# Weight sums of a hybrid decoder block: from loads, VectorE and stores to accumulating DRAM-to-DRAM transfers on GpSimd's queue

## The chip, the core and the metric

The kernel runs on one core of a Trainium2 chip. The metric is the device time of one execution in microseconds. The kernel before takes 1697.17 us, the median of three runs (1697.14 to 1698.39).

The engines are called as the profile calls them: PE (TensorE matmul) and PEld (its weight loads), DVE (VectorE), ACT (ScalarE), POOL (GpSimd) and SP (SyncE). SP, ACT and POOL each have a queue from which transfers (DMAs) are issued in program order; all of them are carried out by the core's 16 DMA engines. "Idle before" and "who waited" in the views are inferred from semaphore events.

## The reference, cut to what matters

One layer of a decoder block on 256 positions of width 2048, in float32: a pre-norm, one wide projection, dilated attention and a gated recurrence side by side, gates, an output projection, and then the feed-forward part, with a normalisation and a residual sum behind each half:

```
a = rmsnorm(h, norm_mix_pre)
proj = a @ w_in                                   # 2048 x 17408
q_a, k_a, v_a, q_r, f_r, i_r, g_r, gate_a, gate_r = split_columns(proj)
attn  = dilated_window_attention(...)             # 3 groups of 8 heads
r_out = hgrn2_chunked(...)                        # 8 heads
y = sigmoid(gate_a) * (attn @ w_attn_branch) + sigmoid(gate_r) * (r_out @ w_hgrn_branch)
h = h + rmsnorm(y @ w_mix_out, norm_mix_post)
a = rmsnorm(h, norm_ffn_pre)
gt, up = split(a @ w_ffn_gate_up)                 # 2048 x 11264
ff = (silu(gt) * up) @ w_ffn_down                 # 5632 x 2048
h = h + rmsnorm(ff, norm_ffn_post)
```

## The kernel before

**Products.** All the large matrix products stream their weights from DRAM. Each weight tile is split into a high and a low part (`hi` on ACT, `lo` on DVE: `raw - hi`), and so are the activations; a product is three matmuls: high by high, high by low, low by high (`prod`, L461).

**Steps and items.** A `Wide` block covers 2 x 512 output columns. It is computed in steps; a step takes 256 rows of the weight, so its `raw` tile is four quarters of 128 x 512 (two row halves k by two column groups g), 1 MB in all, loaded by SP as two DMAs of 512 KB (`load_wide`, L274) into one of three `raw` buffers. `Block`s are narrower; their chunks of 512 KB are loaded by `load_pair` (L262), two to a `raw` buffer. `items` lists all steps and chunks in order of use: 64 steps of the eight early wide blocks (items 0 to 63), 176 chunks, 16 steps of the output projection, 88 of gate and up, 44 of down. The main loop at the end runs over the items: `prepare` (L337) splits the item two ahead and issues loads up to three further `raw` buffers, `multiply` issues the matmuls of this item, and then the evacuations and the side work (`lanes`: attention and recurrence) advance by one piece each. Every engine runs its own queue in the order in which the loop wrote it; nothing but semaphores ties an engine to the item that the loop was at.

**The start.** x (2 MB, in five DMAs) and the first weight tiles are loaded on SP's queue in turn. In the first block the activations of step c + 1 are transposed on PE halfway through step c (`more_x`, L766), and ACT and DVE split them (L617, L621). ACT takes its work in order: the weights of a step, two squares of the norm (L688), then these activations. Between the two sides of a step stand twelve matmuls.

**Seven products.** In some steps a 2 x 2 block product is made with seven products in place of eight (21 matmuls for 24, less adds). It needs four sums of the weight quarters and four sums of the activations (`seven_sums`, L517), and the results are put together in `gather` (L506) and by one add for each output tile when a block is done (L815, L1199, L1405, L1454). With `by7 == 1` the weight sums are made on DVE when the step is split (L434, L440, L441). With `by7 == 2`, which holds for 20 steps of gate and up (`GATE_UP3`, `GATE_UP4`), the sums are made ahead and kept in DRAM, in tiles `presum` of 128 x 2048; `fetch_sums` (L319) loads them four items before their step.

**Sums made ahead.** `weight_sums` (L294) is a generator, advanced once per chunk item by `ahead_of_time` (L327), once the pool `fp` is open and the recurrence doesn't hold it. For each of the 20 jobs it loads the four quarters into an SBUF tile `pre` with two DMAs on SP's queue, makes the sums with four DVE operations (L309, L310, L312, L313), and stores them with one 1 MB DMA on ACT's queue (L316). `make_room` (L1543) finishes what is left of it before the pools of the feed-forward part open.

**POOL.** GpSimd has little to do: it fills constants, issues two small DMAs of `rowg` (L173, L174), and fills the tile `at` of each half of the recurrence with zeros (L987). DVE writes the diagonal of `at` later (L1009).

Of the kernel before, what the change touches and what calls it, by code (L numbers as in the profile page):

```python
# [14 lines left out]
F32 = mybir.dt.float32  # L15
# [3 lines left out]
OP = mybir.AluOpType  # L19

P = 128
# [79 lines left out]
def tile_hybrid_block(ctx: ExitStack, tc: tile.TileContext, t, out):  # L101
    nc = tc.nc
# [12 lines left out]
    def nm(s):  # L115
        serial[0] += 1
        return f"{s}_{serial[0]}"
# [22 lines left out]
    def rsqrt_mean(dst, ss, n, bias=None):  # L140
# [44 lines left out]
    dram = ctx.enter_context(  # L185
        tc.tile_pool(name="dram", bufs=1, space=bass.MemoryType.DRAM, reuse_waits="tile")
    )
# [12 lines left out]
    fp = []  # L200
# [92 lines left out]

    def weight_sums(jobs):  # L294

        for n in jobs:
            x = fp[0].tile([P, 2048], F32, tag="pre", bufs=1, name=nm("pre"))
            b, i = steps[n][:2]
            m = b.order[i][0]
            for g in range(2):  # L300
                nc.sync.dma_start(
                    x[:, g * 1024 : (g + 1) * 1024].rearrange("p (k c) -> p k c", k=2),
                    b.w[2 * m * P : (2 * m + 2) * P, b.cols[g] : b.cols[g] + 512]
                    .rearrange("(k p) c -> p k c", p=P),
                )
            for _ in range(4):
                yield
            r = [x[:, q * 512 : (q + 1) * 512] for q in range(4)]
            nc.vector.tensor_sub(r[2], r[2], r[0])  # L309
            nc.vector.tensor_sub(r[0], r[1], r[0])  # L310
            yield
            nc.vector.tensor_add(r[1], r[1], r[2])  # L312
            nc.vector.tensor_sub(r[3], r[3], r[1])  # L313
            yield
            pre[n] = dram.tile([P, 2048], F32, name=nm("presum"))
            nc.scalar.dma_start(pre[n], x)  # L316
            yield

    def fetch_sums(i):  # L319
        if i < len(items) and items[i][0] is steps:  # L320
# [5 lines left out]

    def ahead_of_time():  # L327

        if fp and back and not hold[0]:
            advance(back)  # L330

    def split(i):
        if i < len(items):
# [67 lines left out]
    def split_wide(n):  # L401

        b, i, raw = steps[n][:3]
        m, by7 = b.order[i]
        prep = b.prep(m, by7) if b.prep else iter(())
        next(prep, None)
        if (b, i) == spare:
            hi = p3("spare", F32R, 2048, 1, "sum")
            lo = Joined(p3("spare", F32R, 1536, 4, "d"), p3("spare", F32R, 512, 4, "d"))
            nc.scalar.activation(hi, raw, AF.Copy)  # L410
            for c in (slice(0, 1536), slice(1536, 2048)):
                nc.vector.tensor_sub(lo[:, c], raw[:, c], hi[:, c].bitcast(F32))
            steps[n][3] = hi, lo
            return
        hi, lo = wslot(), p3("wl", F32R, 2048, 3)
        if not by7:
            for c in (slice(0, 1024), slice(1024, 2048)) if b.halves else (slice(0, 2048),):
                nc.scalar.activation(hi[:, c], raw[:, c], AF.Copy)  # L418
                next(prep, None)
                nc.vector.tensor_sub(lo[:, c], raw[:, c], hi[:, c].bitcast(F32))  # L420
            steps[n][3] = hi, lo
            return
        d = raw[:, 512:]
        if by7 == 2:
            for c, x in zip((slice(0, 1024), slice(1024, 2048)), pre_in.pop(n)):
                nc.scalar.activation(hi[:, c], x, AF.Copy)
                nc.vector.tensor_sub(lo[:, c], x, hi[:, c].bitcast(F32))
            dhi, dlo = p3("dh", F32R, 1536, 4, "d"), p3("dl", F32R, 1536, 4, "d")
            nc.scalar.activation(dhi, d, AF.Copy)
            nc.vector.tensor_sub(dlo, d, dhi.bitcast(F32))  # L430
            steps[n][3] = hi, lo, dhi, dlo
            return
        s = p3("sum", F32, 2048, 1)
        nc.vector.tensor_sub(  # L434
            s[:, :1024].rearrange("p (a c) -> p a c", a=2),
            raw[:, 512:1536].rearrange("p (a c) -> p a c", a=2),
            raw[:, None, :512].to_broadcast([P, 2, 512]),
        )
        nc.scalar.activation(hi[:, :1024], s[:, :1024], AF.Copy)  # L439
        nc.vector.tensor_add(s[:, 1024:1536], raw[:, 512:1024], s[:, 512:1024])  # L440
        nc.vector.tensor_sub(s[:, 1536:], raw[:, 1536:], s[:, 1024:1536])  # L441
        nc.scalar.activation(hi[:, 1024:], s[:, 1024:], AF.Copy)
        next(prep, None)
        dhi, dlo = p3("dh", F32R, 1536, 4, "d"), p3("dl", F32R, 1536, 4, "d")
        nc.scalar.activation(dhi, d, AF.Copy)  # L445
        for c in (slice(0, 1024), slice(1024, 2048)):
            nc.vector.tensor_sub(lo[:, c], s[:, c], hi[:, c].bitcast(F32))  # L447
        next(prep, None)
        nc.vector.tensor_sub(dlo, d, dhi.bitcast(F32))  # L449
        steps[n][3] = hi, lo, dhi, dlo  # L450
# [55 lines left out]
    def gather(b):  # L506
# [7 lines left out]
        nc.vector.tensor_add(e[1, 1], x["p7"], e[1, 1])  # L514
        b.rest = e

    def seven_sums(f, dst):  # L517

        s = ptile("s").rearrange("p (n t) -> p n t", n=4)
        a11, a12, a21, a22 = f[:, 0, :P], f[:, 1, :P], f[:, 0, P:], f[:, 1, P:]  # L520
        for o, x, c, y in ((0, a21, -1.0, a22), (1, s[:, 0, :], -1.0, a11)):
            nc.vector.scalar_tensor_tensor(
                out=s[:, o, :], in0=x, scalar=c, in1=y, op0=OP.mult, op1=OP.subtract
            )
        nc.vector.tensor_sub(s[:, 2, :], a11, a21)
        nc.vector.tensor_sub(s[:, 3, :], a12, s[:, 1, :])
        return (
            lambda: nc.scalar.activation(dst[:, 0], s, AF.Copy),
            lambda: nc.vector.tensor_sub(dst[:, 1], s, dst[:, 0].bitcast(F32)),
        )  # L530
# [120 lines left out]
    def advance(q):  # L651
        if q:
            try:
                next(q[0])
            except StopIteration:
                q.popleft()
                return

    def flush(q):
        while q:  # L660
            advance(q)
# [146 lines left out]
    def totals(b, then):  # L808

        while "r1c" not in ready:  # L810
            yield
        keys = ((0, 0), (0, 1), (1, 0), (1, 1))
        if b.rest:
            for key in keys:
                nc.vector.tensor_add(b.rest[key], b.bank[key], b.rest[key])  # L815
            yield
        for key in keys:
            then(key, b.rest[key] if b.rest else b.bank[key])
            if key == (0, 1):
                yield  # L820
# [374 lines left out]
            nc.scalar.dma_start(hx[j], xv[:, :, j * 512 : (j + 1) * 512])  # L1195

    def mix_sum(j, i, b):
        f = b.rest[i, j % 2]
        nc.vector.tensor_add(f, b.bank[i, j % 2], f)  # L1199

    def mix_square(j, i, b):
        sq = zss[0][:, 4 * i + j : 4 * i + j + 1]
# [197 lines left out]
        turns.append(u)  # L1400

    def evac_ffn(b):
        e, x = b.rest, b.bank
        for key in ((0, 0), (0, 1), (1, 0), (1, 1)):
            nc.vector.tensor_add(e[key], x[key], e[key])  # L1405
            s, g = key
            if g == 0:
                nc.scalar.activation(e[key], e[key], AF.Silu, scale=r2c[:, s : s + 1])
        yield
        for s in range(2):  # L1410
            nc.vector.tensor_mul(e[s, 1], e[s, 1], e[s, 0])
        turns.append([e[0, 1], e[1, 1]])
# [34 lines left out]

    def down_sum(j, i, b):

        f = b.rest[i, j % 2]  # L1450
        nc.vector.tensor_add(f, b.bank[i, j % 2], f)  # L1451

    def down_square(j, i, b):
        sq, r2 = fss[0][:, 4 * i + j : 4 * i + j + 1], r2c[:, i : i + 1]  # L1454
# [88 lines left out]
    def make_room(c):  # L1543
        if c == 2:
            flush(evacs)
            flush(back)
            end_phase1()

    early = [
# [76 lines left out]
    for i in range(len(items)):  # L1626
        kind, n, _ = items[i]
        b, c = kind[n][:2]
        wide = kind is steps
        if wide:  # L1630
            now[0] = b
        if c == 0 and b.pre:
            b.pre()
        if not wide and n in items_pre:
            items_pre[n]()
        if together <= i < together + 5:
            if i == together:
                flush(evacs)
                mix_to_ffn(i)
            continue  # L1640
        if not (wide and b.mid):
            prepare(i)
        if i >= len(items) - 3:
            continue
        multiply(i)
        if b.post:
            b.post(c)
        if wide and c == b.last7:
            gather(b)
        advance(evacs)  # L1650
        if wide and c == b.turn:
            flush(evacs)
            turn_act(turns.popleft())
        for _ in range(2):
            if turns and type(turns[0]) is not list:
                advance(turns)
        advance_lanes()
        if not wide:
            ahead_of_time()
        if c == (len(b.order) if wide else b.steps) - 1:  # L1660
            evacs.append(b.evac(b if wide else b.banks))
            if wide:
                advance(evacs)
# [63 lines left out]
```

## Time and profile before

| what | us |
|---|---|
| median of the runs | 1697.17 |
| profiled execution, from its first to its last instruction (span) | 1695.7 |
| PE busy | 1684.4 |
| DVE busy | 1416.2 |
| ACT busy | 945.6 |
| POOL busy | 3.8 |

Only the span is known of the profiled execution itself; the runs were timed from outside, and their median is 1.5 us above it. PE's matmuls are pipelined, so the busy time of one (some 390 ns for 512 columns) is longer than the step from one to the next; the number of matmuls in a stretch tells the rate. The DMA share is the mean busy share of the 16 DMA engines; in the page it stands at 5 to 8 tenths in most slices.

### The profile page before, as it was taken

To read this page: it belongs to the slowest core of one execution; us is meant where nothing else is said; L and a number is where in the kernel's file an instruction comes from. 1 tells how busy PE (TensorE), PEld (TensorE's weight loads), DVE (VectorE), ACT (ScalarE), POOL (GpSimd) and SP (SyncE) were. 2 spreads that over 40 slices of the span, in tenths; PEclk is the share of its full clock that TensorE was granted. 3 is DMA by queue.
4 is the path that set the end of the run, shared out by engine and by line. 5 is a ranking of instruction groups with operands and counts; after the bars stand their busy time and mean duration, and the time that the engine had idled before them with its cause. 6 is when DMAs were issued, how large, how long until landed. Compare 5 with 4: busy or idle time off the path is not lost.

```text
span 1695.7 us, 21719 instructions
## 1 busy us (share of the span) xinstructions
PE 1684.4 (99%) x8257; PEld 1415.9 (83%) x8257; DVE 1416.2 (84%) x1623; ACT 945.6 (56%) x1080; POOL 3.8 (0%) x13
## 2 busy tenths in 40 slices
PE   9999999999999999999999999999999999999997
PEld 7888888888888888888888888888888888888886
DVE  6999888867978987776668888888888888898987
ACT  6655555544455555555545547555555555665653
POOL 0000000000000000000000000000000000000000
PEclk9999999999999999999999999999999999999999
DMA  8567666669677766788857646777777777777673
GB/s 286 204 224 243 231 232 229 234 216 316 228 250 256 261 239 215 259 310 279 291 171 276 208 165 226 270 249 251 255 254 255 250 248 272 252 269 259 238 255 130
DMA packets 228905, 413.49 MB, mean 244 GB/s; under 512 B 12816, under 2 KB 79552, under 8 KB 226240
## 3 DMA queue, kind: packets, MB, share of 16 engines
q1 hardware_dynamic: 218544, 373.93, 65.6%
q10 hardware_dynamic: 10192, 38.15, 5.9%
q8 instruction: 64, 1.05, 0.3%
q14 instruction: 41, 0.34, 0.1%
q0 software_dynamic: 64, 0.02, 0.0%
HBM read 376.92 MB, written 35.13 MB: 243 GB/s over the span
## 4 chain that ended last, share of the span: by engine, by line
PE 98%; DVE 1%; ACT 0%; issue 0%; DVEq 0%; ACTq 0%
PE acc L138 62%; PE aux L138 34%; PE aux L943 0%; PE aux L610 0%; PE aux L1374 0%; DVE fz L1501 0%; PE acc L1374 0%; DVE wl L420 0%; ACT junk L1455 0%; PE aux L597 0%; DVE e L1451 0%; ACT w L418 0%; PE aux L1136 0%; PE aux L1246 0%; DVE yT L578 0%
## 5 line engine op out<-in xcount | busy, mean ns | idle before, releaser
L138 PE MATMUL acc<-xT,w 128*128 128x256 f32 (+1 forms) x2048 | 365.1, 338 | 0.0
L420 DVE TENSOR_TENSOR wl<-raw,w 128x2048 fp32r<-128x2048 f32 (+1 forms) x140 | 304.6, 2183 | 70.5 <-ACT w L418 68.7
L138 PEld LDWEIGHTS acc<-xT,w 128*128 128x128 f32 x2048 | 311.9, 188 | 44.7
L365 DVE TENSOR_TENSOR w<-raw,w 128x1024 fp32r<-128x1024 f32 x176 | 215.1, 1223 | 118.1 <-ACT w L364 117.5
L418 ACT ACTIVATE w<-raw 128x2048 fp32r<-128x2048 f32 (+1 forms) x140 | 254.6, 1827 | 104.4 <-PE aux L138 33.6
L364 ACT ACTIVATE w<-raw 128x1024 fp32r<-128x1024 f32 x176 | 185.8, 1058 | 191.9 <-PE acc L138 135.8
L138 PE MATMUL acc<-w,xT 128*128 128x512 f32 x578 | 168.8, 391 | 0.0
L439 ACT ACTIVATE w<-sum 128x1024 fp32r<-128x1024 f32 x57 | 60.6, 1062 | 184.8 <-DVE sum L434 177.6
L138 PE MATMUL acc<-w,hT 128*128 128x512 f32 x472 | 152.7, 391 | 0.4 <-DVE hT L1258 0.4
L447 DVE TENSOR_TENSOR wl<-sum,w 128x1024 fp32r<-128x1024 f32 x114 | 137.2, 1221 | 12.8 <-ACT w L439 12.8
L138 PEld LDWEIGHTS acc<-w,xT 128*128 128x128 f32 x578 | 108.2, 188 | 22.2
L138 PE MATMUL aux<-w,hT 128*128 128x512 f32 x374 | 120.0, 389 | 0.0
L449 DVE TENSOR_TENSOR dl<-raw,dh 128x1536 fp32r<-128x1536 f32 x57 | 100.1, 1757 | 14.3 <-ACT dh L445 13.0
L138 PE MATMUL aux<-w,xT 128*128 128x512 f32 x344 | 109.8, 389 | 0.0
L138 PEld LDWEIGHTS acc<-w,hT 128*128 128x128 f32 x472 | 88.5, 188 | 19.0 <-DVE hT L1258 0.9
L138 PE MATMUL acc<-wl,hT 128*128 128x512 f32 x236 | 91.9, 389 | 0.0
L445 ACT ACTIVATE dh<-raw 128x1536 fp32r<-128x1536 f32 x57 | 84.1, 1476 | 8.0 <-PE aux L138 4.4
L138 PE MATMUL acc<-w,a 128*128 128x512 f32 x268 | 83.6, 389 | 0.0
L138 PEld LDWEIGHTS aux<-w,hT 128*128 128x128 f32 x374 | 70.2, 188 | 14.5
L138 PE MATMUL acc<-w,so 128*128 128x512 f32 x240 | 80.8, 391 | 0.0
L138 PE MATMUL aux<-w,a 128*128 128x512 f32 x254 | 79.4, 389 | 0.0
L138 PEld LDWEIGHTS aux<-w,xT 128*128 128x128 f32 x344 | 64.6, 188 | 13.4
(299 smaller groups left out, 2976.2 us busy)
## 6 DMA issues: line engine op xcount, KB each, us to landing
raw<-in_w_in SPq DMA_DIRECT2D x270, 512.0 KB, 4.8
raw<-in_w_ffn_gate_up SPq DMA_DIRECT2D x156, 512.0 KB, 4.9
raw<-in_w_ffn_down SPq DMA_DIRECT2D x88, 512.0 KB, 5.5
pre<-in_w_ffn_gate_up SPq DMA_DIRECT2D x40, 512.0 KB, 6.5
presum<-pre ACTq DMA_DIRECT2D x20, 1024.0 KB, 4.7
s<-presum SPq DMA_DIRECT2D x40, 512.0 KB, 6.9
raw<-in_w_mix_out SPq DMA_DIRECT2D x32, 512.0 KB, 4.8
act<-acts SPq DMA_DIRECT2D x22, 512.0 KB, 6.6
```

The costliest lines, as they stand in the source:

```text
L138: nc.tensor.matmul(ps, lhsT, rhs, start=start, stop=stop, skip_group_check=True)
L364: nc.scalar.activation(wh, raw, AF.Copy)
L365: nc.vector.tensor_sub(wl, raw, wh.bitcast(F32))
L418: nc.scalar.activation(hi[:, c], raw[:, c], AF.Copy)
L420: nc.vector.tensor_sub(lo[:, c], raw[:, c], hi[:, c].bitcast(F32))
L439: nc.scalar.activation(hi[:, :1024], s[:, :1024], AF.Copy)
L445: nc.scalar.activation(dhi, d, AF.Copy)
L447: nc.vector.tensor_sub(lo[:, c], s[:, c], hi[:, c].bitcast(F32))
L449: nc.vector.tensor_sub(dlo, d, dhi.bitcast(F32))
```

## The change

`weight_sums` no longer uses SBUF, DVE, SP or ACT. Each of the 20 jobs is four stages of DMAs on GpSimd's queue, of 128 x 512 (256 KB) each, all from DRAM to DRAM:

- `begin`: four copies of weight quarters into `presum`,
- `first`: two DMAs that add a quarter of the weight to one of `presum`,
- `second` and `third`: one each, adding one quarter of `presum` to another.

The jobs are interleaved: job n's `begin` is issued with job n - 1's `first`, n - 2's `second` and n - 3's `third`, and the next such group eight advances later. The generator is advanced in every item from the ninth on (`i > 7`), wide ones too, so that its instructions are written among items 8 to 191; before, they were written among the chunk items. There are 160 DMAs, 40 MB written.

The scheme of seven products is one whose weight sums are all additions, since the DMAs add. To make up for it `seven_sums` changes signs in the sums of the activations (the same number of operations), and at the end of a block two of the four output tiles are `bank - rest` in place of `bank + rest` (`complete`). The sums made on DVE for `by7 == 1` change from subtractions to additions in the same places. The flush in `make_room` goes.

```diff
     def weight_sums(jobs):
 
-        for n in jobs:
-            x = fp[0].tile([P, 2048], F32, tag="pre", bufs=1, name=nm("pre"))
+        def pieces(n):
             b, i = steps[n][:2]
             m = b.order[i][0]
-            for g in range(2):
-                nc.sync.dma_start(
-                    x[:, g * 1024 : (g + 1) * 1024].rearrange("p (k c) -> p k c", k=2),
-                    b.w[2 * m * P : (2 * m + 2) * P, b.cols[g] : b.cols[g] + 512]
-                    .rearrange("(k p) c -> p k c", p=P),
-                )
-            for _ in range(4):
+            return [
+                b.w[(2 * m + k) * P : (2 * m + k + 1) * P, b.cols[g] : b.cols[g] + 512]
+                for g, k in product(range(2), repeat=2)
+            ]
+
+        def begin(n):
+            r = pieces(n)
+            x = pre[n] = dram.tile([P, 2048], F32, name=nm("presum"))
+            for at, q in ((0, 0), (1, 1), (2, 0), (3, 3)):
+                nc.gpsimd.dma_start(x[:, at * 512 : (at + 1) * 512], r[q])
+
+        def first(n):
+            r, x = pieces(n), pre[n]
+            nc.gpsimd.dma_start(x[:, :512], r[1], accum_op=OP.add)
+            nc.gpsimd.dma_start(x[:, 1024:1536], r[2], accum_op=OP.add)
+
+        def second(n):
+            x = pre[n]
+            nc.gpsimd.dma_start(x[:, 512:1024], x[:, 1024:1536], accum_op=OP.add)
+
+        def third(n):
+            x = pre[n]
+            nc.gpsimd.dma_start(x[:, 1536:], x[:, 512:1024], accum_op=OP.add)
+
+        stages = (begin, first, second, third)
+        for at in range(len(jobs) + 3):
+            for lag in (3, 2, 1, 0):
+                if 0 <= at - lag < len(jobs):
+                    stages[lag](jobs[at - lag])
+            for _ in range(8):
                 yield
-            r = [x[:, q * 512 : (q + 1) * 512] for q in range(4)]
-            nc.vector.tensor_sub(r[2], r[2], r[0])
-            nc.vector.tensor_sub(r[0], r[1], r[0])
-            yield
-            nc.vector.tensor_add(r[1], r[1], r[2])
-            nc.vector.tensor_sub(r[3], r[3], r[1])
-            yield
-            pre[n] = dram.tile([P, 2048], F32, name=nm("presum"))
-            nc.scalar.dma_start(pre[n], x)
-            yield
...
     def ahead_of_time():
 
-        if fp and back and not hold[0]:
-            advance(back)
+        advance(back)
...
+    def complete(b, key):
+
+        add_to = nc.vector.tensor_add if key[1] else nc.vector.tensor_sub
+        add_to(b.rest[key], b.bank[key], b.rest[key])
...
         a11, a12, a21, a22 = f[:, 0, :P], f[:, 1, :P], f[:, 0, P:], f[:, 1, P:]
-        for o, x, c, y in ((0, a21, -1.0, a22), (1, s[:, 0, :], -1.0, a11)):
-            nc.vector.scalar_tensor_tensor(
-                out=s[:, o, :], in0=x, scalar=c, in1=y, op0=OP.mult, op1=OP.subtract
-            )
+        nc.vector.tensor_sub(s[:, 0, :], a22, a21)
         nc.vector.tensor_sub(s[:, 2, :], a11, a21)
-        nc.vector.tensor_sub(s[:, 3, :], a12, s[:, 1, :])
+        nc.vector.scalar_tensor_tensor(
+            out=s[:, 1, :], in0=s[:, 0, :], scalar=-1.0, in1=a11, op0=OP.mult, op1=OP.subtract
+        )
+        nc.vector.tensor_add(s[:, 3, :], a12, s[:, 1, :])
...
         if c == 2:
             flush(evacs)
-            flush(back)
             end_phase1()
...
         advance_lanes()
-        if not wide:
+        if i > 7:
             ahead_of_time()
```

In the order of the instructions, POOL's queue before reads as follows from its last constants on to its end. `rowg` holds three small vectors, `at` is the tile of the recurrence; the brackets name the semaphores that an instruction waits for (DMAHW: earlier DMAs of SP and ACT; Activation, DVE, PE: those engines).

```order
L170 MEMSET eps 128x1
L173 DMA rowg<-in_norm_ffn_pre 16x128
L174 DMA rowg<-in_hgrn_lower_bounds 16x128
L987 MEMSET at_3359 128x1024 [waits DMAHW6_49,DMAHW4_49,DMAHW7_49,DMAHW2_49,Activation_49]
L987 MEMSET at_4554 128x1024
L1723 UNCONDITIONAL_BRANCH
```

In the change the same place reads as follows (DMASW: earlier DMAs of POOL's own queue, eight semaphores in turn; each `presum` is a job).

```order
L170 MEMSET eps 128x1
L173 DMA rowg<-in_norm_ffn_pre 16x128
L174 DMA rowg<-in_hgrn_lower_bounds 16x128
L308 DMA presum_660<-in_w_ffn_gate_up 128x512 x4
L312 DMA presum_660<-in_w_ffn_gate_up 128x512 [waits DMASW2_49]
L313 DMA presum_660<-in_w_ffn_gate_up 128x512 [waits DMASW4_49]
L308 DMA presum_963<-in_w_ffn_gate_up 128x512 [waits DMASW0_49]
L308 DMA presum_963<-in_w_ffn_gate_up 128x512 [waits DMASW1_49]
L308 DMA presum_963<-in_w_ffn_gate_up 128x512
L308 DMA presum_963<-in_w_ffn_gate_up 128x512 [waits DMASW3_49]
L317 DMA presum_660<-presum_660 128x512 [waits DMASW7_49]
```

The four copies of the first job stand right behind the DMAs of `rowg` and wait for nothing; what follows waits for POOL's own DMAs alone. Further on in POOL's queue, the first fill of `at` now stands behind 81 of the 160 DMAs, and 40 more stand between it and the second fill:

```order
L313 DMA presum_3198<-in_w_ffn_gate_up 128x512 [waits DMASW1_49]
L308 DMA presum_3395<-in_w_ffn_gate_up 128x512
L308 DMA presum_3395<-in_w_ffn_gate_up 128x512 [waits DMASW0_49]
L308 DMA presum_3395<-in_w_ffn_gate_up 128x512
L308 DMA presum_3395<-in_w_ffn_gate_up 128x512 [waits DMASW2_49]
L1003 MEMSET at_3421 128x1024 [waits DVE_49,PE_49]
L321 DMA presum_3002<-presum_3002 128x512 [waits DMASW4_49,DMASW3_49]
```

So the fills, which stood next to each other, moved behind the transfers, and the transfers behind the fills wait for them. On SP's queue the 40 loads of `pre` are gone from among the loads of chunks, and nothing else moved:

```order
-L269 DMA raw_2758<-in_w_in 128x4x256 x2
-L301 DMA pre_2789<-in_w_ffn_gate_up 128x2x512 x2
-L269 DMA raw_2814<-in_w_in 128x4x256 x2
-L269 DMA raw_2867<-in_w_in 128x4x256 x2
-L269 DMA raw_2912<-in_w_in 128x4x256 x2
-L301 DMA pre_2963<-in_w_ffn_gate_up 128x2x512 x2
```

These are rows of before as the difference prints them; the loads of `raw` stand in the change too, in the same order under other numbers. PE's order of matmuls and weight loads is the same row for row.

More of the change, by code (lines that the diff above doesn't have):

```diff
@@ L433, in split_wide @@
         s = p3("sum", F32, 2048, 1)
-        nc.vector.tensor_sub(
+        nc.vector.tensor_add(
             s[:, :1024].rearrange("p (a c) -> p a c", a=2),
@@ L440, in split_wide @@
         nc.vector.tensor_add(s[:, 1024:1536], raw[:, 512:1024], s[:, 512:1024])
-        nc.vector.tensor_sub(s[:, 1536:], raw[:, 1536:], s[:, 1024:1536])
+        nc.vector.tensor_add(s[:, 1536:], raw[:, 1536:], s[:, 1024:1536])
         nc.scalar.activation(hi[:, 1024:], s[:, 1024:], AF.Copy)
@@ L814, in totals @@
             for key in keys:
-                nc.vector.tensor_add(b.rest[key], b.bank[key], b.rest[key])
+                complete(b, key)
             yield
@@ L1197, in mix_sum @@
     def mix_sum(j, i, b):
-        f = b.rest[i, j % 2]
-        nc.vector.tensor_add(f, b.bank[i, j % 2], f)
+        complete(b, (i, j % 2))
     def mix_square(j, i, b):
@@ L1402, in evac_ffn @@
     def evac_ffn(b):
-        e, x = b.rest, b.bank
+        e = b.rest
         for key in ((0, 0), (0, 1), (1, 0), (1, 1)):
-            nc.vector.tensor_add(e[key], x[key], e[key])
+            complete(b, key)
             s, g = key
@@ L1448, in down_sum @@
     def down_sum(j, i, b):
-        f = b.rest[i, j % 2]
-        nc.vector.tensor_add(f, b.bank[i, j % 2], f)
+        complete(b, (i, j % 2))
     def down_square(j, i, b):
```

## The prediction

> **What bounds the kernel now.** I read the page first: the span, the busy shares, and the chain that ended last.
>
> ```profile
> span 1695.7 us, 21719 instructions
> PE 1684.4 (99%) x8257; PEld 1415.9 (83%) x8257; DVE 1416.2 (84%) x1623; ACT 945.6 (56%) x1080; POOL 3.8 (0%) x13
> ...
> PE 98%; DVE 1%; ACT 0%; issue 0%; DVEq 0%; ACTq 0%
> ```
>
> PE is busy for all but 11.3 us of the span, and 98% of the chain is its own matmuls. The view of waits, for PE alone, says what there is to save:
>
> ```profile
> PE aux L138 <- DVE warm L162: 1.2, 1, 1.2
> PE acc L138 <- DVE hT L1258: 0.4, 1, 0.4
> PE acc L138 <- DVE gate L1173: 0.2, 1, 0.2
> PE aux L943 <- DVE p L937: 0.2, 1, 0.2
> ```
>
> After the first 1.2 us PE waits 0.8 us for anything. Relief for DVE, ACT or SP can bring that much at the most. So the question is only whether the change makes PE wait where it does not now, and by its nature it can do so through the DMA engines. The third view is busy time by stretch; the last columns are the granted clock, the DMA share and GB/s.
>
> ```profile
> 0.00:5.00 5.00, 3.81 (x10) 1.28 (x11) 0.27 (x1) 1.28 (x1) 2.00 (x11) 1.00 0.56 177
> 5.00:10.00 5.00, 5.00 (x23) 3.54 (x24) 3.15 (x8) 3.56 (x8) 0.00 (x0) 1.00 0.96 319
> 10.00:15.00 5.00, 5.00 (x24) 4.13 (x23) 3.72 (x5) 2.92 (x4) 0.00 (x0) 1.00 1.05 393
> 15.00:20.00 5.00, 5.00 (x25) 3.99 (x24) 3.33 (x4) 3.59 (x9) 0.00 (x0) 1.00 1.05 387
> 20.00:25.00 5.00, 5.00 (x26) 4.13 (x25) 3.75 (x8) 4.77 (x9) 0.00 (x0) 1.00 1.05 384
> 25.00:30.00 5.00, 5.00 (x26) 4.15 (x25) 3.07 (x7) 3.31 (x11) 0.00 (x0) 1.00 0.88 288
> 60.00:345.00 285.00, 285.00 (x1259) 236.00 (x1258) 252.02 (x221) 159.86 (x133) 0.00 (x0) 1.00 0.66 225
> 350.00:850.00 500.00, 499.85 (x2947) 437.89 (x2946) 388.91 (x566) 262.68 (x396) 0.15 (x1) 1.00 0.77 261
> ```
>
> From 5 to 25 us the DMA engines are full: 384 to 393 GB/s at a share of 1.05. Later a third of them is free (share 0.66 from 60 to 345 us, 0.77 from 350 to 850 us). So a transfer more costs nothing on average, but in the ramp every byte more puts back a byte of x or of the first weights. The timelines of the ramp show how little room there is (start, duration, engine, operation, and in brackets the idle time before it and what ended it):
>
> ```profile
> 14.40 1.06 ACT L418 ACTIVATE w<-raw 128x1024 fp32r<-128x1024 f32 x1 [1.65 <-DMA raw<-in_w_in]
> 19.88 1.06 ACT L418 ACTIVATE w<-raw 128x1024 fp32r<-128x1024 f32 x1 [1.12 <-DMA raw<-in_w_in]
> 21.17 1.07 ACT L418 ACTIVATE w<-raw 128x1024 fp32r<-128x1024 f32 x1 [0.23 <-DMA raw<-in_w_in]
> 22.14 0.62 ACT L688 ACTIVATE junk<-x 128x512 f32<-128x512 f32 x1
> 23.36 0.82 ACT L617 ACTIVATE xT<-aux,colg 128x256 fp32r<-128x256 f32 x2
> 24.21 0.88 DVE L621 SCALAR_TENSOR_TENSOR xT<-aux,colg,xT 128x256 fp32r<-128x256 f32 x2
> 28.56 0.60 PE L610 MATMUL aux<-ident,x 128*128 128x128 f32 x4
> ```
>
> ACT waits for weights three times. From the landing at 21.17 it works without a gap to the activations of step 3 (to 24.18), and DVE has their low parts at 25.09. The transposes at 28.56 stand halfway through step 3, twelve matmuls behind its start; a matmul takes 285 / 1259 = 0.226 us, so step 3 starts at 25.85, and its third matmul, the first with a low part of x, at 26.3. The slack is 26.3 - 25.1 = **1.2 us**: a landing later than that stops PE.
>
> **What goes.** The rows of the tile `pre`:
>
> ```profile
> L301 SPq DMA_DIRECT2D pre<-in_w_ffn_gate_up x40: 367/467/507, 357.6 to 819.5; - x40
> L309 DVE TENSOR_TENSOR pre<-pre x20: 680/685/695, 366.5 to 828.3; 128x512 f32<-128x512 f32 x20
> L310 DVE TENSOR_TENSOR pre<-pre x20: 691/692/694, 367.2 to 829.0; 128x512 f32<-128x512 f32 x20
> L312 DVE TENSOR_TENSOR pre<-pre x20: 678/684/702, 369.0 to 833.0; 128x512 f32<-128x512 f32 x20
> L313 DVE TENSOR_TENSOR pre<-pre x20: 691/692/695, 369.7 to 833.7; 128x512 f32<-128x512 f32 x20
> L316 ACTq DMA_DIRECT2D presum<-pre x20: 326/326/327, 373.0 to 835.3; - x20
> ```
>
> DVE loses 20 x (0.685 + 0.692 + 0.684 + 0.692) = 55 us, SP 40 x 0.47 = 19 us of issue, ACT 20 x 0.33 = 7 us. All of it lies between 357 and 836 us, where PE is busy for 499.85 of 500 us: worth **0 us** (0.2 at most).
>
> **What only changes its sign.** The rows above price an add (L312, 0.684) like a subtraction (L309, 0.685), so `complete` and the sums of `by7 == 1` cost nothing. In `seven_sums` two plain operations, an add or subtract each, and two with a scalar become three and one; they are as many and as long:
>
> ```profile
> 34.09 0.29 DVE L522 SCALAR_TENSOR_TENSOR s<-f 128x128 f32<-128x128 f32 x1
> 34.62 0.28 DVE L525 TENSOR_TENSOR s<-f 128x128 f32<-128x128 f32 x1
> ```
>
> **What comes: 160 DMAs on POOL's queue, and when.** `i > 7` decides where they are written, not when they are issued. No instruction ahead of them in POOL's queue waits for PE, DVE or ACT, and they wait only for one another. POOL's own timeline says when it is free:
>
> ```profile
> 1.51 0.62 POOL L173 DMA_DIRECT2D rowg<-in_norm_ffn_pre  x1
> 2.12 0.48 POOL L174 DMA_DIRECT2D rowg<-in_hgrn_lower_bounds  x1
> 348.31 1.84 POOL L987 MEMSET at<- 128x1024 f32 x2 [345.70 <-ACT v L842]
> ```
>
> So the first 81 start at 2.6 us, in the ramp, and not behind the first block; then the first fill of `at` waits to about 348 us, and the other 79 follow it.
>
> *Their pace.* No row shows a POOL DMA of 128 rows, from DRAM to DRAM, or one that adds. The nearest rows: issue of 16 rows on POOL took 0.48 to 0.62 us, which by rows would be 8 x 0.62 = 4.9 us for 128. Landings (KB of one, median us) of 256 KB, of a small one of POOL, and of half a load of weights:
>
> ```profile
> waits<-e ACTq DMA_DIRECT2D x24, 256.0 KB, 3.4
> raw<-in_w_ffn_gate_up SPq DMA_DIRECT2D x20, 256.0 KB, 3.1
> rowg<-in_norm_ffn_pre POOLq DMA_DIRECT2D x1, 8.0 KB, 3.6
> raw<-in_w_in SPq DMA_DIRECT2D x270, 512.0 KB, 4.8
> ```
>
> In a group of eight DMAs one wait counts: `first` waits for the third copy of the `begin` issued just ahead. Eight issues of 0.6 to 1 us and a landing of 3.4 us, some two to three times that when the engines are full, make 8 to 16 us a group, 1 to 2 us a DMA. I take 2 us, near the full-engine end, since that is the state here; the ends are 0.6 us (nothing but issue) and 4.9 us.
>
> *The ramp.* Allowing 2 us to the first byte, POOL moves data from about 4.5 us on. At 2 us each it puts some 12 DMAs of 0.262 MB, 3.1 MB, among the loads until the weights of step 3 have landed, which then takes until about 29 us. At 388 GB/s that is a delay of 8.1 us; less the slack of 1.2 us PE stands **7 us**. At 4.9 us a DMA it is four of them, 2.7 us of delay and 1.5 us of idle. At the other end POOL takes every second turn all the time: what SP moved between 4.5 and 21.2 us, 16.7 us long, takes twice that, and PE stands 15.5 us.
>
> A rule of the Trainium skill bears on this end ("DMA: Bandwidth & Descriptors", section "Queues, rings and completion order"): each DMA engine takes its queues in turn, packet by packet, whoever issued first. By it the 15.5 us would hold as long as POOL's queue always has a packet ready; no row here shows two full queues side by side. I stay at 7 us because of the waits inside each group.
>
> *Behind the ramp.* To 345 us the engines have 0.34 of 285 us free. The 69 DMAs left of the first burst are 18 MB, 47 us of full engines; at 2 us each they spread over 138 us, in which 47 us are free. If adding takes an engine twice as long they need 70 us, 23 us too many, of which the three `raw` buffers (three steps of 24 x 0.226 = 5.4 us, less the landing of 4.8 us) cover some 11. So 0 to 12 us; I take **2 us**, since POOL's queue slows itself when the engines are full. Behind 348 us the 42 MB that `pre` and `presum<-pre` moved from 350 to 850 us, a third of the 130 MB there, are gone, so there is more room: **0 us**.
>
> *Sum*: 1695.7 + 7 + 2 = 1704.7 us of span. The median of the runs stands 1.5 us above the span of the profiled execution; with that **1706 us**.
>
> **Rivals.**
>
> *A, not slower: POOL's queue only trickles in the ramp.* If a DMA of 128 rows occupies POOL for long, few get in before step 3. PE stands under 3.4 us (0.2%, about what a measurement of this kernel can tell from no change) if the delay is under 4.6 us, that is 1.8 MB or 7 DMAs in some 21.5 us: the mechanism decides from about 3.1 us a DMA. For it: 16 rows take 0.6 us, so 128 could take 4.9. Against it: SP issues the 256 rows of 2 KB of one load of `pre` in 0.47 us (L301 above). It gives 1697 to 1700 us.
>
> *B: equal turns, and adding is dear.* The ramp costs 15.5 us and the first burst 12 us: 1695.7 + 27.5 + 1.5 = 1725 us. For it: a share of 1.05 leaves nothing over in the ramp. Against it: the waits inside each group.
>
> *C: the fill of `at` comes too late.* DVE needs it at 434 us:
>
> ```profile
> L1009 DVE COPY_PREDICATED at<-ident,aux x4: 735/741/747, 434.2 to 566.9; 128x512 f32<-128x512 int32 x4
> ```
>
> 81 DMAs have 431 us, so this decides from 5.3 us a DMA on. Behind the waiting DVE stand the splits of the weights, and PE waits for those. At 6 us the fill comes at 489 us: 55 us lost, 1752 us. Against it: even 4.9 us is in time.
>
> *D: faster.* Only if the matmuls themselves went quicker, for which no row speaks; the waits that could go are 0.8 us.
>
> **How the numbers follow.** The forecast (1701 to 1716) has 0.50, A 0.29, B 0.15, C 0.04, D 0.02. The range reaches over A, from 1696.5, and to B's 1727; C, D and the far part of B are left out. Slower by over 0.2%: forecast, B and most of C, 0.69 with rounding; within 0.2%: A, 0.29; faster: 0.02.
>
> **What would show it.** POOL's first DMA at 2.6 us and the 81st well before 348 us; in the stretches from 5 to 35 us a share of 1.0 throughout, ACT's waits for `raw` longer, and PE with under 5 us busy in some of them; the idle of PE in the ramp close to the whole difference; from 60 to 200 us a higher DMA share with PE full. PE full in the ramp, or a first POOL DMA after 54 us, would make the prediction wrong, and so would PE idle near 434 us.

## The result, and the profile after

The change made the kernel slower: 1769.58 us, the median of four runs (1766.07 to 1773.63), against 1697.16 us before; ratio 1.0426 (95% interval 1.041 to 1.0442). The forecast was 1706 us, with a range up to 1727. The sign was forecast, and so was that POOL's DMAs delay the loads of weights at the start; that they go on delaying them through both bursts was not. The loss is 72 us in place of 9.

The page of the change, its first lines, its chain and its DMA queues (packets, MB, share of the 16 engines over the span):

```profile
span 1771.8 us, 21763 instructions
PE 1709.8 (97%) x8257; PEld 1423.2 (80%) x8257; DVE 1367.2 (77%) x1543; ACT 946.4 (53%) x1080; POOL 113.5 (6%) x173
...
q1 hardware_dynamic: 207664, 352.96, 59.7%
q0 software_dynamic: 17984, 41.97, 10.7%
...
PE 80%; DMA 13%; DVE 3%; ACT 2%; issue 1%; SPq 1%; DVEq 0%; ACTq 0%
```

The chain, which was PE for 98%, now has DMA for 13%: loads of weights. PE has as many matmuls, but the span is 76.1 us longer: PE's busy time grew by 25.4 us and its idle time by 50.7. POOL's own queue, q0, moved 42 MB. When it did so, its timeline says:

```profile
2.70 2.12 POOL L308 DMA_DIRECT2D presum<-in_w_ffn_gate_up  x4
...
159.94 0.53 POOL L308 DMA_DIRECT2D presum<-in_w_ffn_gate_up  x1 [0.41 <-issue]
395.09 0.96 POOL L1003 MEMSET at<- 128x1024 f32 x1 [234.62 <-PE acc L138]
...
563.05 0.81 POOL L321 DMA_DIRECT2D presum<-presum  x1 [7.18 <-DMA presum<-presum]
```

Two bursts: 81 DMAs from 2.7 to 160 us (2.0 us each) and 79 from 396 to 563 us (2.1 us). PE's time is lost in just these. The view by stretch, the change first and then before (the numbers behind x are instructions, the last three columns the granted clock, DMA share and GB/s):

```profile
0.00:60.00 60.00, 41.16 (x155) 29.01 (x156) 19.71 (x34) 21.91 (x40) 22.69 (x43) 0.86 1.00 287
60.00:120.00 60.00, 49.68 (x201) 37.85 (x200) 39.00 (x55) 28.59 (x36) 19.79 (x29) 0.94 1.04 278
120.00:180.00 60.00, 49.59 (x195) 38.01 (x195) 40.87 (x37) 23.95 (x20) 13.87 (x21) 0.94 0.97 277
180.00:240.00 60.00, 58.70 (x258) 48.14 (x257) 54.62 (x49) 32.77 (x26) 0.00 (x0) 1.00 0.71 251
420.00:480.00 60.00, 56.05 (x301) 47.87 (x300) 30.20 (x39) 22.77 (x30) 21.47 (x31) 0.94 1.08 288
```

```profile
60.00:120.00 60.00, 60.00 (x266) 49.68 (x265) 54.71 (x49) 36.13 (x31) 0.00 (x0) 1.00 0.59 201
180.00:240.00 60.00, 60.00 (x267) 49.67 (x266) 51.88 (x47) 35.10 (x31) 0.00 (x0) 1.00 0.68 228
```

From 60 to 120 us PE gets through 201 matmuls in place of 266, with the engines at a share of 1.04. From 180 us on, with the first burst over, it is nearly back at its rate. Two more rows date the loss. They are the first and the last start of the matmuls of the chunks, before and in the change:

```profile
L138 PE MATMUL acc<-xT,w x2048: 274/337/497, 345.8 to 751.4; 128*128 128x512 f32 x94, 128*128 128x256 f32 x93
```

```profile
L138 PE MATMUL acc<-xT,w x2048: 274/393/628, 403.2 to 826.8; 128*128 128x512 f32 x94, 128*128 128x256 f32 x93
```

So **57.4 us** are lost by the first chunk (first burst), and 75.4 by the last: **18.0 us** in the second burst. Comparing the start of the same matmul in both traces in the same way, the lag is 10.3 us where before was at 25 us, 28.7 us where it was at 60 us.

The DMA view of 60 to 170 us, the change first and then before:

```profile
q0 software_dynamic: 5892, 13.97, 57.3%
q1 hardware_dynamic: 8243, 16.12, 44.2%
...
raw<-in_w_in SPq DMA_DIRECT2D x30, 512.0 KB, 14.4
```

```profile
q1 hardware_dynamic: 11281, 21.92, 58.4%
...
raw<-in_w_in SPq DMA_DIRECT2D x42, 512.0 KB, 4.8
```

POOL's queue has 57% of the engines, SP's 44% where it had 58%; a load of weights lands 14.4 us after its issue, where before it took 4.8. SP moves 16.12 MB in 110 us, 147 GB/s, in place of 21.92 MB, 199 GB/s. A packet of SP's queue held its engine for about as long as before (share x 16 engines x 110 us, divided by the packets: 94 ns against 91). So the engines did not work more slowly on the loads; the loads had less of the engines' time.

### The profile page after: what moved, and what is told of

Read it like the earlier page. It is cut to its first block, busy times and chain, and to the rows that moved or that the text cites. A ratio compares the mean times of both kernels' runs of the same rounds, so it can differ in the third digit from the quotient of the medians.

```text
span 1771.8 us, 21763 instructions
## 1 busy us (share of the span) xinstructions
PE 1709.8 (97%) x8257; PEld 1423.2 (80%) x8257; DVE 1367.2 (77%) x1543; ACT 946.4 (53%) x1080; POOL 113.5 (6%) x173
## 3 DMA queue, kind: packets, MB, share of 16 engines
q0 software_dynamic: 17984, 41.97, 10.7%
## 4 chain that ended last, share of the span: by engine, by line
PE 80%; DMA 13%; DVE 3%; ACT 2%; issue 1%; SPq 1%; DVEq 0%; ACTq 0%
PE acc L138 49%; PE aux L138 29%; DMA raw<-in_w_in 13%; DVE wl L431 1%; ACT w L375 1%; DVE w L376 1%; ACT w L429 0%; PE aux L959 0%; ACT dh L456 0%; DVE dl L460 0%; PE aux L1389 0%; DVE fz L1515 0%; DVE e L531 0%; SPq L269 0%; PE acc L1389 0%
## 5 line engine op out<-in xcount | busy, mean ns | idle before, releaser
L138 PE MATMUL acc<-xT,w 128*128 128x256 f32 (+1 forms) x2048 | 372.4, 341 | 10.0 <-DVE w L376 5.3
L138 PE MATMUL acc<-w,xT 128*128 128x512 f32 x578 | 174.1, 400 | 16.3 <-ACT xT L633 15.3
L138 PE MATMUL acc<-wl,xT 128*128 128x512 f32 x193 | 77.4, 401 | 2.3 <-DVE wl L431 2.3
```

The lines of the kernel that those rows point to most:

```text
L138: nc.tensor.matmul(ps, lhsT, rhs, start=start, stop=stop, skip_group_check=True)
```

## The experiments

Unless another is named, each kernel is the change with the edit shown. The lag is, as above, the later start of the same matmul against before.

**The signs alone** (`e_signs`). The sums are made as before, by loads, DVE and stores, with additions:

```diff
-            nc.vector.tensor_sub(r[2], r[2], r[0])
-            nc.vector.tensor_sub(r[0], r[1], r[0])
+            nc.vector.tensor_add(r[2], r[2], r[0])
+            nc.vector.tensor_add(r[0], r[1], r[0])
...
-            nc.vector.tensor_sub(r[3], r[3], r[1])
+            nc.vector.tensor_add(r[3], r[3], r[1])
```

> The scheme with plus signs alone: the sums are made by loads, DVE and stores as before, with additions, and POOL issues none of it. All theories: the signs cost nothing, 1696.5 to 1698 us. If it is slower by more than 1 us, a part of the loss is in the other operations (complete, seven_sums).

1697.3 us; ratio 0.9999 (0.999 to 1.0008). The signs cost nothing; all of the loss is in POOL's DMAs.

**No adding** (`e_copy`).

```diff
-            nc.gpsimd.dma_start(x[:, :512], r[1], accum_op=OP.add)
-            nc.gpsimd.dma_start(x[:, 1024:1536], r[2], accum_op=OP.add)
+            nc.gpsimd.dma_start(x[:, :512], r[1])
+            nc.gpsimd.dma_start(x[:, 1024:1536], r[2])
```

(and so in `second` and `third`)

> The 80 adding DMAs are plain copies of the same size, with the same waits in the same order (the sums are left out, so the output is not the reference's). Theory 'turns': a packet of a copy takes 159 ns for 4096 bytes in the change's trace and one of an add 176 ns for 2048, so POOL's work falls from about 190 to about 115 us of full engines, and the loss with it from 74 to 35 to 50 us: 1732 to 1748 us. Theory 'adding': without adds nothing is disturbed, 1697 to 1705 us. Theory 'start': four copies still go first and the ramp is lost as now; 1755 us or more.

1775.31 us, one run, of a kernel that leaves the sums out: no faster than with adds. Adding is not the cause, but my own number missed as well. Its queue and its chunk matmuls:

```profile
q0 software_dynamic: 12864, 41.97, 7.6%
```

```profile
L138 PE MATMUL acc<-xT,w x2048: 274/392/628, 391.1 to 828.5; 128*128 128x512 f32 x94, 128*128 128x256 f32 x93
```

Copies are indeed cheaper for the engines: 7.6% of 1773.5 us is 135 us, against 10.7% of 1771.8, 190 us, with adds. The first burst is shorter and costs 45.3 us in place of 57.4. But the second costs 31.8 us in place of 18.0. The queue does not use less of the engines at a time when its DMAs are cheaper; it runs faster. In the second burst the copies had 58.6% of the engines and left SP's loads 41.8% (383 to 500 us), where with adds it was 56.2% and 50.5% (396 to 563 us); this goes with the larger loss, but why the copies got more is open.

**Hold the first DMA** (`e_hold`). Only the first group waits for the ninth item, through a small tile that DVE fills and POOL fills again:

```diff
         for at in range(len(jobs) + 3):
+            if at == 0:
+                gate = cpool.tile([P, 8], F32, tag="gate", bufs=2, name=nm("gate"))
+                nc.vector.memset(gate, 0.0)
+                nc.gpsimd.memset(gate, 0.0)
```

> Only the first group waits for a fill that DVE makes in the ninth item (about 50 us); from there the queue runs free as in the change. Theory 'turns': the burst of 81 DMAs lies from some 50 to 210 us and takes its 57% of the engines there from loads that need 0.66 of them: about 40 us lost, and 18 us in the second burst as now: 1745 to 1760 us. Theory 'start': the ramp is undisturbed, so only the 18 us of the second burst stay: 1712 to 1718 us. Theory 'adding': as now, 1760 to 1770 us.

1757.21 us, one run. The lag is nothing until the burst begins (its first DMA is issued at 66 us), 47.2 us at the first chunk, and 59 at the end. The ramp is not what makes the loss; a burst among the wide steps costs nearly as much. "Start" falls.

**The written place** (`e_late`): `if i > 63:` in place of `if i > 7:`.

> The generator is advanced from item 64 on in place of item 8, so that all its instructions are written among the chunks, as the sums were before. Theory 'turns' with a queue that nothing holds: the first DMA is still issued at 2.7 us; some 25 stand ahead of the first fill of the recurrence's tile and take 50 us of the start (20 to 25 us lost), and some 135 follow that fill at about 370 us as one burst of some 280 us (0.11 us lost per us as now, 30 us): 1745 to 1755 us. Rival 'place' (a DMA is issued about where it is written): none before 330 us, 1697 to 1717 us.

1759.78 us, one run. The first DMA is issued at 2.70 us as in the change, and PE lags 21.4 us by 60 us; a second burst from 360 us brings the rest (61.7 us in all). That is above the 1745 to 1755 us of "turns": the second burst cost 40 us, not 30. The place in the loop doesn't hold the queue.

**Pace the groups** (`e_paced`): the fill of `e_hold` ahead of every group, without the `if`.

> Every group of eight DMAs now stands behind a small fill on POOL that waits for a fill written on DVE in the same item, so that the groups are issued at the pace of the items (one in some 41 us among the early wide steps, one in some 22 us among the chunks) and not as one burst. Theory 'turns' (POOL's packets take the DMA engines in turn with SP's, whatever SP needs; the loss is the burst): 23 groups of about 9 us of full engines each (0.573 x 110 us for 50 DMAs is 1.26 us a DMA) find room between 0.66 and 1.0 in the early steps, and just about room among the chunks: 1697 to 1703 us. Theory 'adding' (the read-modify-write itself slows the other transfers, paced or not): as many adds, so at least half of the loss stays, 1735 us or more. Theory 'start' (the stalls of the ramp are the cause and what follows is their consequence): 1697 to 1700 us too.

1739.14 us; ratio 1.0243 (1.0226 to 1.026). Over half of the loss is still there, and it is a miss for "turns". The groups were where they should be (66, 105, 149 us and so on), yet from the third to the seventh each cost 6 to 9 us, among the wide steps. Behind the third, in the views by stretch and of ACT's timeline:

```profile
150.00:155.00 5.00, 5.00 (x23) 4.14 (x23) 3.48 (x3) 2.78 (x3) 2.56 (x4) 1.00 1.02 291
165.00:170.00 5.00, 5.00 (x24) 4.13 (x23) 1.46 (x2) 0.17 (x1) 0.00 (x0) 1.00 1.03 394
170.00:175.00 5.00, 1.79 (x7) 0.94 (x5) 4.82 (x5) 4.67 (x4) 0.00 (x0) 1.00 0.48 185
```

```profile
169.83 1.06 ACT L453 ACTIVATE w<-sum 128x1024 fp32r<-128x1024 f32 x1 [9.19 <-DVE sum L448]
```

The engines are full from 150 to 170 us, the sums of a weight tile come late, and then PE stands. A group of eight holds the engines for about 20 us, which is longer than the weights are loaded ahead. Just before, the engines stood nearly idle (a share of 0.15 at 145 to 150 us), so there was room on average, but not within those 20 us. Among the chunks the sixteen groups left cost under 6 us together, 3.7 of it behind one of them.

**Pace single DMAs** (`e_spread`): one DMA per item, each behind a fill.

```diff
+        def gated():
+            gate = cpool.tile([P, 8], F32, tag="gate", bufs=2, name=nm("gate"))
+            nc.vector.memset(gate, 0.0)
+            nc.gpsimd.memset(gate, 0.0)
...
-                    stages[lag](jobs[at - lag])
-            for _ in range(8):
+                    for _ in stages[lag](jobs[at - lag]):
+                        left -= 1
+                        yield
+                        gated()
+            for _ in range(left):
```

(the stages yield behind each DMA; each group begins with a fill, and `left` starts at 8)

> As e_paced, but every single DMA of POOL stands behind a fill that waits for DVE, and the generator is left after each, so that one DMA of 256 KB is issued per item in place of eight in every eighth item. e_paced lost 5 to 6 us a group among the wide steps and under 1 us a group among the chunks, with the engines full for some 20 us behind each group and the loads of weights landing after up to 18 us. Theory 'short burst' (a stall comes when POOL holds the engines for longer than the weights are loaded ahead, some 8 us; not from the bytes or the adds): a DMA is 1.1 to 1.6 us of full engines, an early item leaves 0.34 x 5.2 = 1.8 us free and a chunk item some 1.3 us: 1697 to 1701 us. Theory 'adding' (the cost belongs to each add): as e_paced, 1735 us or more.

1705.2 us; ratio 1.004 (1.0027 to 1.0054). Of the change's 72 us, 8 are left, with the same transfers and adds; that is still 4 us above what "short burst" said.

**More fills in flight** (`e_spread16`): `bufs=16` for `gate`.

> e_spread with 16 buffers for the small fills in place of 2, so that DVE's fill never waits for POOL's fill of two items before. In e_spread PE lost 4 us from 250 to 345 us and 3.5 us from 560 to 610 us, with DVE's fill named as releaser in three of PE's waits and ACT waiting 34 us for raw. If the rest was the fills (DVE held up behind a POOL that waits for its own DMAs): 1697 to 1699 us. If it is the loads (one DMA per wide step still makes some of them late): 1701 to 1705 us.

1703.27 us; ratio 1.0037 (1.0024 to 1.0049). All that is left is lost among the wide steps, between 200 and 350 us; the loss near 600 us is gone. The stretch, here and before:

```profile
170.00:345.00 175.00, 170.70 (x747) 139.31 (x746) 147.07 (x162) 93.61 (x78) 25.45 (x68) 1.00 0.87 266
```

```profile
170.00:345.00 175.00, 175.00 (x774) 144.91 (x773) 151.67 (x134) 95.17 (x79) 0.00 (x0) 1.00 0.68 228
```

With a share of 0.87 the engines are not full on average, and some loads still come late; ACT waits 25 us for `raw` of w_in in this kernel and 6 us before. But the views name DVE's fill for four of PE's waits (4.1 us), nearly all of the 4.8 us by which PE's idle time is above that of before. So late loads and the fills aren't told apart here; the time lies in the range that was said for the loads.

**Pace the groups, among the chunks** (`e_paced_late`): `e_paced` with `if i > 63:`.

> As e_paced (a group of eight for every eight items), but the generator is advanced from item 64 on, among the chunks only. In e_paced the lag of PE grew by some 36 us among the wide steps (11 groups or fewer) and by 5.6 us among the chunks. Theory 'short burst': a chunk's packets and its 512 KB are half as big and a group costs little there, but now eleven groups more fall on chunks, one in 22 us with 9 us of full engines: 1702 to 1715 us. If groups cost 5 to 6 us here too: 1735 us or more.

1698.43 us, one run, beside 1697.47 before: the lag grows by 1.1 us in the first hundred us of the chunks, and not at all behind them. Better than I expected: eight at a time cost next to nothing here. Why the chunks bear what the wide steps do not was not tested. Behind the group at 394 us, three slices of 5 us from 400 us on had shares of 0.97, 1.06 and 0.96, where in `e_paced` the engines were full for 20 us.

**The same, unpaced** (`e_hold_late`): `e_hold` with `if i > 63:`. The same DMAs, begun in the same item as in `e_paced_late`, but left free.

> The control for e_paced_late: the same 160 DMAs written among the chunks, the first held by a fill until item 64, and then left free in place of paced by groups. Theory 'turns' (what costs is that POOL's queue never pauses while the loads are wanted): a burst of some 160 x 2.1 = 336 us from 345 us on, at 0.11 us lost for each of its us as in the second burst of the change: 1725 to 1740 us. Rival 'chunks' (e_paced_late lost nothing because chunks have room, paced or not): 1697 to 1702 us.

1747.25 us, one run: 49 us lost, and so even more than "turns" said. The DMA view from 350 to 680 us:

```profile
q0 software_dynamic: 17902, 41.88, 56.7%
q1 hardware_dynamic: 47952, 48.76, 48.1%
...
raw<-in_w_in SPq DMA_DIRECT2D x90, 512.0 KB, 16.2
```

and that of `e_paced_late` from 345 to 910 us:

```profile
q1 hardware_dynamic: 81753, 99.28, 52.7%
q0 software_dynamic: 17776, 41.69, 35.5%
...
raw<-in_w_in SPq DMA_DIRECT2D x136, 512.0 KB, 7.9
```

Bytes, adds and place are the same in both. Left free, POOL's queue has 57% of the engines and a load of weights lands after 16.2 us; paced, it has 36%, and the load lands after 7.9 us, early enough.

**Jobs one after the other** (`e_seq`). No fill, no interleaving: each stage waits for the landing of the one before.

```diff
-        stages = (begin, first, second, third)
-        for at in range(len(jobs) + 3):
-            for lag in (3, 2, 1, 0):
-                if 0 <= at - lag < len(jobs):
-                    stages[lag](jobs[at - lag])
+        for n in jobs:
+            for stage in (begin, first, second, third):
+                stage(n)
```

> Nothing holds POOL's queue, but the jobs are not interleaved: each job's four copies, two adds, add and add wait for one another, so POOL is kept back by its own landings (three in a row in a job, of some 6 to 8 us). Theory 'turns' (POOL takes its turns whenever it has a packet, so its share of the engines is set by its own waits): some 30 us for a job in place of 16, a share of 0.3 in place of 0.57, which mostly fits beside 0.66: the ramp loses 5 to 15 us and the rest 0 to 15 us, 1705 to 1730 us. Theory 'adding' or 'bytes' (the same transfers cost the same however they are spread): 1760 us or more.

1730.92 us, one run, just above the upper end of "turns" and far from what "bytes" said. A job took some 26 us (first copies at 2.7, 27.8 and 54.2 us), and POOL had 38% of the engines from 60 to 300 us. The ramp lost 6.1 us, the other wide steps 27, where 15 at most was said, and the chunks nothing.

**Single DMAs among the chunks** (`e_spread16_late`): `e_spread16` with `if i > 63:`.

> The same, one DMA per item, written among the chunks only (from item 64). The chunks took eight DMAs at a time with 1 us lost in all (e_paced_late), so single ones cost nothing: 1696.5 to 1698.5 us, no more than before and no less, since DVE's 55 us that are saved stand beside a PE that is always busy. Rival: the relief of DVE, SP and ACT among the chunks brings something: under 1694 us.

1697.66 us; ratio 1.0002 (0.9993 to 1.0011). No version beat the kernel before; this one equals it, without the SBUF tile and with DVE busy for 47 us less (1369.2 us: 80 operations on `pre` are gone, 183 short fills came), which gains nothing beside PE.

## Why the prediction was wrong

**What goes: right.** It was priced at 0 us. `e_spread16_late`, which has all of the removal and none of the harm, is the same as before within 0.1%.

**The signs: right**, 0 us by `e_signs`.

**When the DMAs are issued: right.** The first at 2.70 us, the 81st at 160 us, and `e_late` shows that the written place doesn't matter until something in POOL's queue waits for a compute engine.

**Their pace: right**, 2.0 us a DMA where I took 2; a DMA of POOL's landed after 7.7 us from 60 to 170 us, 2.3 times the 3.4 of the nearest row, as "two to three times that" had it.

**The ramp: right in mechanism, too small.** ACT's waits for weights in the change:

```profile
22.96 1.06 ACT L429 ACTIVATE w<-raw 128x1024 fp32r<-128x1024 f32 x1 [6.99 <-DMA raw<-in_w_in]
37.63 1.06 ACT L429 ACTIVATE w<-raw 128x1024 fp32r<-128x1024 f32 x1 [9.51 <-DMA raw<-in_w_in]
```

The lag was 10.3 us about where step 3 starts, against 7 forecast and an upper bound of 15.5. But I let the loss end there. The ramp's own need was not over, the burst was not either, and at 60 us of before the lag was 28.7. PE's idle time in the ramp was not close to the whole difference either: PE stood for 18.8 of the first 60 us, against 50.7 us more of idle time in all.

**Behind the ramp: this is the step that failed.** I had weighed the engine time needed (47 or 70 us) against the 47 us free, with up to 12 us lost, and then took 2 us, "since POOL's queue slows itself when the engines are full". It did not: it kept the 2 us a DMA that I had taken, at a share of 1.04, and it was SP's loads that slowed. A queue that never paused took 56 to 57% of the engines in both bursts and in `e_hold_late`, whatever the loads needed. So the free time of the average is no bound on the loss. From 60 to 170 us SP's loads had 44.2% of the engines, where before they used 58.4%, with PE full. 44.2 / 58.4 is 0.76, and from 60 to 120 us PE got through 201 / 266 = 0.76 of its matmuls. Over these 110 us that makes 0.24 x 110 = 27 us, of the 57 of the first burst. This sum sets the share beside the loss; it does not say why the share is 57%.

The same mistake made **0 us** of the second burst, which cost 18; that the old transfers are gone there helps on average only. Among the chunks the sum of shares gives too little: in `e_hold_late` the loads had 48.1% from 350 to 680 us, where `e_paced_late` used 52.6% for the same steps (350 to 631 us) with PE nearly full. That is a ratio of 0.91, or 28 us of the 330, and 49 were lost. What makes the rest stays open. That it is the missing pause which costs is shown by `e_hold_late` against `e_paced_late`: 49 us and 1 us for the same transfers.

**Not priced at all: PE's clock.** The view by stretch, in three stretches of the change:

```profile
26.00:32.80 6.80, 4.99 (x12) 3.74 (x13) 2.10 (x3) 2.12 (x7) 1.58 (x3) 0.50 1.10 255
39.70:46.50 6.80, 3.01 (x7) 2.25 (x8) 2.85 (x8) 3.00 (x7) 2.35 (x4) 0.50 1.06 214
53.30:56.70 3.40, 2.83 (x7) 2.07 (x8) 2.45 (x7) 1.93 (x5) 0.82 (x1) 0.50 0.96 174
```

The granted clock stands at one half in them, and in three more stretches of some 6.8 us from 101, 132 and 466 us on: 37.5 us in all. The same matmuls kept PE busy for 25.4 us longer over the whole run. When they are compared one by one with before, those that fall into these stretches make some 15 us of it, a fifth of the loss. Some 8 us more lie in matmuls just ahead of a gap, which no later one overlaps. PE's longest waits just ahead of the six stretches were 4.5 us (to 27.8), 7.2 us (to 43.5), and then 2.8, 3.0, 2.1 and 1.8 us. The Trainium skill ("TensorE: Matmul & The Clock Gate", Part 1) says that the array falls to half its clock after an idle window of some 3.4 us and needs a busy one to come back. The trace agrees in the length of the stretches, 3.4 or 6.8 us, but not in the wait: four of the six came behind waits shorter than 3.4 us. No experiment kept the clock up in a stall, so this share is read from the trace only.

**Rival B had the turns**, "equal turns, and adding is dear", at 0.15, and 1725 us, but only for the ramp. Its 12 us for the first burst behind the ramp rested on dear adds, which were not needed (`e_copy`), and so its price was too low. The rule cited from the Trainium skill ("DMA: Bandwidth & Descriptors", "Queues, rings and completion order"), that each engine takes its queues in turn, agrees with shares of 57 and 44%; whether the turns go by packets no run here could tell. **Rival A** (a trickle) was out with the first burst's pace. **Rival C** needed the fill by 434 us; it came at 395 us, and DVE wrote the diagonal only at 504, about as late as PE was by then. Where PE stood near 434 us, the chain names loads of weights. **Rival D** had nothing to gain, as `e_spread16_late` shows.

## What to carry to other kernels

A DMA queue whose instructions wait only for each other is not where you wrote it: here it started at once and took more than half of the DMA engines (56 to 59% in the bursts shown), however much the loads that feed the bound engine needed. Background transfers need a pace, such as a wait on a compute engine ahead of each portion, and the portion must be small enough for the place: among the wide steps a group of eight cost 6 to 9 us and single DMAs still 6 us in all, among the chunks groups of eight cost next to nothing. Judge room by the worst stretch as long as the loads run ahead, not by the mean share; and price a stall of PE with the clock that it may cost behind it.

## What the runs showed of the hardware that was not expected

- An adding DMA from DRAM to DRAM costs the engines more than a copy: 190 against 135 us of all 16 engines in bursts of the same 42 MB, 80 of 160 DMAs being adds. So an add cost 55 / 80 = 0.7 us of full engines more than a copy of its 256 KB; without the adds the time was no shorter.
- POOL issues a DMA of 128 rows in about 0.5 us (four in 2.12 us), no more than one of 16 rows (0.52 and 0.66 us); an add takes about 0.8 us.
- A load of 512 KB that lands after 4.8 us in the kernel before took 14 to 16 us beside a second queue that never paused, some three times as long with 44 to 48% of the engines left to SP's queue.
